# Encoder layer with two kinds of attention on one core: half strips in chunk two's projection, and local heads' scores and values held behind 512-column runs

## The chip, the core and the metric

The kernel runs on one core of a Trainium2 chip. The metric is the device time in microseconds (us); the median of several runs counts. TensorE (PE, with PEld for its weight loads), VectorE (DVE), ScalarE (ACT), GpSimd (POOL) and SyncE (SP, which issues the transfers here) each work through their own list of instructions in order.

## What is computed

```python
u = rms_norm(h, norm_w) @ w_in
qa, ka, va, za, qb, kb, vb, zb = split(u)
qa, ka = rope(rms_norm(qa, q_norm_a)), rope(rms_norm(ka, k_norm_a))
ya = global_gqa(qa, ka, va) * silu(za)                    # 8 heads, 2 of keys and values, all tokens
qb, kb = rms_norm(qb, q_norm_b), rms_norm(kb, k_norm_b)
yb = neighbourhood_attention(qb, kb, vb, rpb) * silu(zb)  # 8 heads, a window of 8 x 16 tokens and 16 meta tokens
return h + concatenate([ya, yb]) @ w_out
```

`h` has 2048 columns; there are a prompt of 1024 tokens and a sample of 256, each with the same 16 meta tokens in front. All inputs are float32.

## The kernel before

A float32 product is made of three matmuls of two-part operands: high by high, high by low, low by high. The input projection goes by **strips** of 128 output columns, 52 in all. A strip has 2048 / 128 = 16 steps `kt` over the input columns, and they are taken in four **quarters** `c` of four steps (`WCH = 4`). `strips` (from line 191) loads a quarter's weights (`wr`), splits them into `wh` and `wl` (ScalarE casts, VectorE subtracts; for some strips the low part is read back from an earlier chunk), and then issues its matmuls. `wh` and `wl` have four buffers each, `wr` three.

The tokens go through in two chunks. Chunk one has 512 tokens, one block. Chunk two (`chunk2`) has 784 tokens in two blocks: 512 columns (tile `x`) and 272 columns (tile `xb`). Per quarter each block has 4 steps x 3 = 12 matmuls, so that TensorE goes back and forth: 12 matmuls of 512 columns, 12 of 272, 12 of 512, and so on, four times a strip. Each block of a strip adds up in its own PSUM tile `pp` (four buffers), and is evacuated by `qk_evac`, `v_rows` or `z_evac`.

Among the strips of chunk two stands attention. First come the global heads (tiles `sp<-q,kf` for scores, `po<-ph,va` for values), issued by `run` behind the strips that they need; a strip of a local head follows each. Then come the other local strips, and in them the local heads: at the end of every second quarter, `run_due` issues what a table of places has for it, at most one block's scores (`scores`: lines 488, 315, 316) and one block's values (`values`: lines 519, 522), both in `attend_strip`. A block's values have their place two half strips behind its scores. Between them lie the masked scores on VectorE (L493), maxima (L502, L505, L326, and GpSimd L328), exponentials on ScalarE (L510, L513) and the meta tokens' probabilities `Pm` (L337, L338).

The order in which all of this stands on each engine is made by a scheduler that models the time of the instructions and keeps dependencies; `place_after` and `add_manual_dep` add an order where no data asks for one. The last strip of chunk two is **turned** (`self.turn`): its 272-column block goes first in each quarter. `tie` names the quarter and block behind which the transposes of the strip before (`v_turn`, `rows_out`, L543) may stand. Behind chunk two comes the output projection (`outproj`, lines 1073 to 1075), with the last local head's blocks in it.

Of the kernel before, what the change touches and what calls it, by code (L numbers as in the profile page):

```python
# [21 lines left out]
P = 128  # L22
# [26 lines left out]
WCH = 4  # L49
# [10 lines left out]
class Kern:  # L60
# [131 lines left out]
    def strips(self, jobs, getx):  # L192


        nc, tc = self.nc, self.tc
        out = [[pool.tile([P, 512], F32, tag=tag, name="pp") for pool, tag in pools] for _, _, pools in jobs]
        for c in range(KT // WCH):
            ws = []
            behind = self.behind.pop(0) if self.behind else None
            for j, (s, _, _) in enumerate(jobs):  # L200
                wp = self.w if j < 2 else self.w1
                with tc.high_priority(offset=self.woff), tc.issue_after(behind) if behind else nullcontext():
                    w = self.raw.tile([P, WCH, P], F32, tag="raw", name="wr")
                    cuts = ((0, 1), (1, WCH)) if self.projected == 3 and c == 0 and not self.second else ((0, WCH),)
                    for i, e in cuts:
                        self.lastw = nc.sync.dma_start(w[:, i:e], self.io["w_in"][s][:, c * WCH + i:c * WCH + e, :]).ins
                    wh = wp.tile([P, WCH, P], F32R, tag="wh", name="wh")
                    wl = wp.tile([P, WCH, P], F32R, tag="wl", name="wl")
                    if self.second and s not in AGAIN:
                        nc.sync.dma_start(wl[:].bitcast(F32), self.wld[s][:, c * WCH:(c + 1) * WCH, :])  # L210
                        nc.scalar.copy(wh[:], w[:])
                    else:
                        for i, e in cuts:
                            self.lastsplit = self.split(wh[:, i:e], wl[:, i:e], w[:, i:e])
                            self.lasthi = self.hi
                ws.append((wh, wl))
                if not self.second and s not in AGAIN:
                    nc.sync.dma_start(self.wld[s][:, c * WCH:(c + 1) * WCH, :], wl[:].bitcast(F32))
            nb = len(jobs[0][1])
            for b in range(nb)[::-1] if self.turn else range(nb):  # L220
                for k in range(WCH):
                    kt = c * WCH + k
                    xh, xl = getx(kt)[b]
                    first, last = kt == 0, kt == KT - 1
                    for (wh, wl), ps, (_, blocks, _) in zip(ws, out, jobs):
                        p, n = ps[b], blocks[b][1]
                        nc.tensor.matmul(p[:, :n], wh[:, k, :], xh[:, :n], start=first, stop=False)  # L227
                        nc.tensor.matmul(p[:, :n], wh[:, k, :], xl[:, :n], start=False, stop=False)  # L228
                        self.lastmm = nc.tensor.matmul(p[:, :n], wl[:, k, :], xh[:, :n], start=False, stop=last).ins  # L229
                if self.turned and (c, b) == self.tie:  # L230
                    for i in self.turned:
                        tc.add_manual_dep(i, self.lastmm.name, mybir.DependencyInfo(
                            mybir.DependencyClass.NoSync, mybir.DependencyReason.DATA), reason="turned")
                    self.turned = []
            if c % 2:
                self.run_due()
        return out

    def turn_ins(self, i):
        self.turned.append(i)  # L240

    def run_due(self):
        if self.late:
# [222 lines left out]
    def attend_strip(self, q, qf, zs, k, meta, vals, vmeta, tab, w, ydst):  # L466

        nc = self.nc  # L470
        qv = q[:].rearrange("p i (g r) -> p i g r", g=4)[:, :, :, 64 * w:64 * w + 64]
        qfv = qf[:].rearrange("p (g r) -> p g r", g=4)[:, :, 64 * w:64 * w + 64]
        groups = {0: (0, 2), 3: (2, 4), 1: (0, 3), 2: (1, 4)}
        pa = self.sp.tile([P, 2, QB], F32, tag="sp", name="sp")
        pb = self.sp.tile([P, 2, QB], F32, tag="sp", name="sp")
        sa = self.s.tile([P, 2, QB], F32, tag="S", name="S")
        sb = self.s.tile([P, 2, QB], F32, tag="S", name="S")
        pa, pb, sa, sb = (x[:].rearrange("p a b -> p (a b)") for x in (pa, pb, sa, sb))

        def part(a, b, t):  # L480

            return (a[:, :P], b[:, :192], b[:, 192:384], a[:, P:2 * P])[t]

        for t in (0, 3, 1, 2):
            a, e = groups[t]
            dst = part(pa, pb, t)
            o = 256 * t + 32 * WIN0[w]
            nc.tensor.matmul(dst, k[:, o:o + P], qfv[:, a:e, :], start=True, stop=True)  # L488
            if t == 3:
                sm = self.meta_scores(pa[:, 256:], meta, qv[:, 0], qv[:, 1], SCALE)  # L490
        ty = WTYPE[w]
        for x, y, n, o in ((sa, pa, 256, 64), (sb, pb, 384, 0)):
            nc.vector.scalar_tensor_tensor(out=x[:, :n], in0=y[:, :n], scalar=SCALE, in1=tab[:, ty, o:o + n],  # L493
                                           op0=ALU.mult, op1=ALU.add)

        def ap(t, off, dims):
            return bass.AP(t.tensor, t.offset + off, [list(t.ap[0])] + dims)

        def gather(name, op):

            m = self.t.tile([P, QB], F32, tag="t", name=name)
            nc.vector.tensor_tensor(out=ap(m[:], 0, [[128, 2], [64, 2], [1, 64]]), in0=ap(sa, 0, [[128, 2], [64, 2], [1, 64]]),  # L502
                                    in1=ap(sb, 0, [[128, 2], [192, 2], [1, 64]]), op=op)
            v = ap(m[:], 64, [[64, 2], [1, 64]])
            nc.vector.tensor_tensor(out=v, in0=v, in1=ap(sb, 64, [[192, 2], [1, 64]]), op=op)  # L505
            return m

        ma = self.all_max(gather("m1", ALU.max), sm)
        nc.vector.tensor_tensor(out=sa[:, :256], in0=sa[:, :256], in1=ma[:], op=ALU.subtract)
        nc.scalar.activation(sa[:, :256], sa[:, :256], AF.Exp)  # L510
        v = ap(sb, 0, [[192, 2], [1, 192]])
        nc.vector.tensor_tensor(out=v, in0=v, in1=ap(ma[:], 0, [[64, 2], [1, 192]]), op=ALU.subtract)
        nc.scalar.activation(sb[:, :384], sb[:, :384], AF.Exp)  # L513
        pm3 = self.meta_probs(sm, ma, 1.0)
        tot = self.mx.tile([P, 2, QB], F32, tag="mx", name="tot")[:, 0, :]
        self.all_sum(gather("a1", ALU.add), sm, tot)
        yield
        po = self.op.tile([P, 2, QB], F32, tag="po", name="po")[:, 0, :]
        nc.tensor.matmul(po, vmeta, pm3[:], start=True, stop=False)
        for t in (0, 3, 1, 2):  # L520
            a, e = groups[t]
            nc.tensor.matmul(po[:, 64 * a:64 * e], vals[:, t, :], part(sa, sb, t), start=False, stop=t == 2)  # L522
        self.put_y(po, tot, zs, ydst)
# [103 lines left out]
    def chunk1(self):  # L627
        nc, io = self.nc, self.io
        self.early_due, self.place = {}, 0
        self.due, self.late, self.turn, self.behind, self.turned, self.tie = iter(()), [], False, [], [], (1, 0)  # L630
        self.woff, self.second, self.projected, self.sums = 0, False, 0, self.w_sums()
        self.scale2 = [self.one2.tile([P, T2], F32, tag=n, name=n) for n in ("rb2", "eb2")]
        self.xsq, self.vlcopies, self.wouts = {}, [], 0
        self.start_chunk(T1)
# [102 lines left out]
        for g in range(2):  # L737
# [4 lines left out]
            else:  # L742
                k, = pr(k_strip(KA + g, g, kw, True))
# [6 lines left out]
        for h in range(8):  # L750
            kj, qj = kb_strip(KB + h, 2 + h, kwb), qb_strip(QB_ + h, 8 + h, qwb)
            k, = pr(kj)
# [15 lines left out]
    def chunk2(self):  # L768
        nc, io = self.nc, self.io
# [29 lines left out]
        def v_rows_of(s, g):  # L799

            def evac(ps):
                for p, (o, n) in zip(ps, BL):
                    self.rows_out(self.v_rows(p, o, n), n, self.vn[g], C1P + o)
            return s, BL, evac
# [141 lines left out]
        for g in range(2):  # L946
            if g == 0:
                k, _ = pr(k_strip(KA, 0, kw, True), v_rows_of(VA, 0))
                self.tie = 0, 1
            else:  # L950
                k, = pr(k_strip(KA + g, g, kw, True))
                pr(v_rows_of(VA + g, g))
            v = v_tiles(g)
            for h in range(4 * g, 4 * g + 4):
                z, = pr(z_strip(ZA + h, h) + (((self.sp, "sp"),) if h == 0 else ()))
                q, = pr(q_strip(QA + h, h, qw, True))
                run(h, q, z, k, v)
                fill(FILL)
# [390 lines left out]
```

## Time and profile before

| | |
|---|---|
| median of 3 runs | 2153.4 us (2153.36 to 2154.49) |
| profiled execution | 2154.02 us, its span 2152.2 us |
| TensorE busy | 2146.3 us |
| VectorE busy | 1675.4 us |
| ScalarE busy | 1204.0 us |
| GpSimd busy | 530.0 us |
| chain that ended last | 99% TensorE |

A matmul's row gives its start and how long it was in the engine. Neighbours overlap there, so the time that one takes from the engine is the distance from its start to the start of the next. A row with several instructions (x4, x8) has them merged.

### The profile page before, as it was taken

Reading aid. Unit: us, or ns where it says so; the run is one execution under the profiler, and the core shown is the slowest. Engines: PE = TensorE matmul, PEld = TensorE weight load, DVE = VectorE, ACT = ScalarE, POOL = GpSimd, SP = SyncE. Lnnn points to the kernel's source line nnn. Section 1 sums busy time; section 2 is a strip of 40 time slices with the busy share of each in tenths; the row PEclk is TensorE's granted clock in tenths of the full one; section 3 lists DMA queues with packets and bytes.
Section 4 is the critical chain, followed back from the end, with each engine's and each line's share of the span. In section 5 each row is a group of like instructions: output and inputs, shape, how many; then the busy total and the mean of one; then the engine's idle time right before and its main releaser. Section 6 shows DMA issues by size and latency. Waiting matters only on the chain.

```text
span 2152.2 us, 33487 instructions
## 1 busy us (share of the span) xinstructions
PE 2146.3 (100%) x11473; PEld 1866.0 (87%) x11473; DVE 1675.4 (78%) x3053; ACT 1204.0 (56%) x2459; POOL 530.0 (25%) x250
## 2 busy tenths in 40 slices
PE   9999999999999999999999999999999999999999
PEld 7888888888888899998998898989999888888887
DVE  7688987788874899898799898787787886545763
ACT  7677644554665777777677776444444454232230
POOL 1142422222221223232133413333333311000000
PEclk9999999999999999999999999999999999999999
DMA  8657799988654333334333334654433364762663
GB/s 294 215 186 228 242 295 319 348 280 271 212 190 133 99 100 108 109 108 125 100 105 101 106 119 128 206 162 139 133 123 124 114 214 144 241 235 89 235 226 107
DMA packets 257419, 377.21 MB, mean 175 GB/s; under 512 B 43072, under 2 KB 108768, under 8 KB 257248
## 3 DMA queue, kind: packets, MB, share of 16 engines
q1 hardware_dynamic: 257248, 375.07, 54.2%
q8 instruction: 90, 1.47, 0.3%
q14 instruction: 81, 0.66, 0.1%
HBM read 281.01 MB, written 100.38 MB: 177 GB/s over the span
## 4 chain that ended last, share of the span: by engine, by line
PE 99%; DMA 0%; DVE 0%; SPq 0%; issue 0%; ACT 0%
PE pp L227 22%; PE pp L229 22%; PE pp L228 22%; PE pq L1075 6%; PE pq L1074 6%; PE pq L1073 6%; PE po L422 3%; PE po L522 2%; PE sp L488 2%; PE sp L383 2%; PE sp L384 2%; PE sp L382 1%; PE po L423 1%; PE tp L543 0%; PE sm_ps L316 0%; PE sm_ps L315 0%
## 5 line engine op out<-in xcount | busy, mean ns | idle before, releaser
L227 PE MATMUL pp<-x,wh 128*128 128x512 f32 (+1 forms) x1664 | 654.4, 394 | 0.8 <-ACT wh L66 0.8
L228 PE MATMUL pp<-x,wh 128*128 128x512 f32 (+1 forms) x1664 | 648.3, 390 | 0.0
L229 PE MATMUL pp<-x,wl 128*128 128x512 f32 (+1 forms) x1664 | 648.2, 390 | 0.0
L229 PEld LDWEIGHTS pp<-x,wl 128*128 128x128 f32 x1664 | 312.6, 188 | 63.0 <-DVE wl L67 0.6
L227 PEld LDWEIGHTS pp<-x,wh 128*128 128x128 f32 x1664 | 312.6, 188 | 57.8 <-ACT wh L66 3.1
L228 PEld LDWEIGHTS pp<-x,wh 128*128 128x128 f32 x1664 | 312.9, 188 | 53.6
L262 POOL PARTITION_ALL_REDUCE m<-ms x78 | 237.8, 3049 | 324.5 <-ACT ms L260 251.2
L346 POOL PARTITION_ALL_REDUCE tot<-a x80 | 175.8, 2198 | 476.2 <-DVE a L343 449.2
L67 DVE TENSOR_TENSOR wl<-wr,wh 128x512 fp32r<-128x512 f32 (+2 forms) x287 | 212.6, 742 | 102.4 <-ACT wh L66 77.3
L66 ACT CAST wh<-wr 128x512 fp32r<-128x512 f32 (+2 forms) x287 | 174.0, 611 | 163.9 <-PE pp L228 148.9
L228 PE MATMUL pp<-xb,wh 128*128 128x272 f32 x832 | 240.6, 289 | 0.0
L227 PE MATMUL pp<-xb,wh 128*128 128x272 f32 x832 | 239.7, 288 | 0.0
L229 PE MATMUL pp<-xb,wl 128*128 128x272 f32 x832 | 239.4, 288 | 0.0
L1075 PE MATMUL pq<-wm,yl 128*128 128x512 f32 x560 | 218.5, 390 | 0.1
L1073 PE MATMUL pq<-wm,yh 128*128 128x512 f32 x560 | 218.5, 390 | 0.0
L1074 PE MATMUL pq<-wm,yh 128*128 128x512 f32 x560 | 218.2, 390 | 0.0
L328 POOL PARTITION_ALL_REDUCE ma<-m x80 | 109.1, 1364 | 424.7 <-DVE m L326 424.7
L228 PEld LDWEIGHTS pp<-xb,wh 128*128 128x128 f32 x832 | 156.5, 188 | 8.4
L227 PEld LDWEIGHTS pp<-xb,wh 128*128 128x128 f32 x832 | 156.6, 188 | 8.1
L229 PEld LDWEIGHTS pp<-xb,wl 128*128 128x128 f32 x832 | 157.5, 189 | 0.9
L1075 PEld LDWEIGHTS pq<-wm,yl 128*128 128x128 f32 x560 | 105.1, 188 | 22.3 <-DVE yl L67 0.5
L1073 PEld LDWEIGHTS pq<-wm,yh 128*128 128x128 f32 x560 | 105.2, 188 | 21.7
(217 smaller groups left out, 3879.3 us busy)
## 6 DMA issues: line engine op xcount, KB each, us to landing
wr<-in_w_in SPq DMA_DIRECT2D x413, 256.0 KB, 3.4
wld<-wl SPq DMA_DIRECT2D x132, 256.0 KB, 4.2
wl<-wld SPq DMA_DIRECT2D x132, 256.0 KB, 3.1
yr<-yd SPq DMA_DIRECT2D x35, 512.0 KB, 5.2
wq<-in_w_out SPq DMA_DIRECT2D x64, 256.0 KB, 5.1
td<-wq SPq DMA_DIRECT2D x64, 256.0 KB, 4.3
ww<-td SPq DMA_DIRECT2D x64, 256.0 KB, 5.4
ww<-in_w_out SPq DMA_DIRECT2D x48, 256.0 KB, 5.1
```

The lines of the kernel that those rows point to most:

```text
L66: self.hi = nc.scalar.copy(hi, full).ins
L67: return nc.vector.tensor_tensor(out=lo, in0=full, in1=hi.bitcast(F32), op=ALU.subtract).ins
L227: nc.tensor.matmul(p[:, :n], wh[:, k, :], xh[:, :n], start=first, stop=False)
L228: nc.tensor.matmul(p[:, :n], wh[:, k, :], xl[:, :n], start=False, stop=False)
L229: self.lastmm = nc.tensor.matmul(p[:, :n], wl[:, k, :], xh[:, :n], start=False, stop=last).ins
L262: nc.gpsimd.partition_all_reduce(m2[:], ms[:], P, RED.add)
L328: nc.gpsimd.partition_all_reduce(ma[:], m1[:], P, RED.max)
L346: nc.gpsimd.partition_all_reduce(tot[:], a1[:], P, RED.add)
L422: nc.tensor.matmul(po[:], vh, hl[:, i], start=j == 0, stop=False)
L1073: nc.tensor.matmul(ps, yh, wh, start=k == 0, stop=False)
L1074: nc.tensor.matmul(ps, yh, wl, start=False, stop=False)
L1075: self.lastmm = nc.tensor.matmul(ps, yl, wh, start=False, stop=k == 7).ins
```

## The change

In `strips`, a lone job with two blocks (chunk two's strips, the turned one excepted) no longer issues matmuls at an even quarter: it keeps the quarter's weights in `held`, and at the odd quarter goes through both quarters for the 512-column block, then through both for the 272-column block. So 24 matmuls of 512 columns are followed by 24 of 272.

`hold` takes note of instructions, outside the turned strip: the four windows' score matmuls of a local block (not the meta tokens' ones) and the first of its values' matmuls. In chunk two, behind the next 512-column run, `place_after` ties them to its last matmul, so that they stand behind it. `tie` becomes quarter 0, block 0 once the first strips are done, where it was block 1.

```diff
@@ strips
+        held = []
         for c in range(KT // WCH):
@@
             nb = len(jobs[0][1])
+            held.append((c, ws))
+            if nb > 1 and len(jobs) == 1 and c % 2 == 0 and not self.turn:
+                continue
             for b in range(nb)[::-1] if self.turn else range(nb):
-                for k in range(WCH):
-                    kt = c * WCH + k
+                for kt, ws in [(d * WCH + k, w) for d, w in held for k in range(WCH)]:
+                    k = kt % WCH
                     xh, xl = getx(kt)[b]
@@
-                if self.turned and (c, b) == self.tie:
+                if b == 0 and self.second and not self.turn:
+                    for i in self.held:
+                        self.place_after(i, self.lastmm, "whole run")
+                    self.held = []
+                if self.turned and (held[0][0], b) == self.tie:
@@
                     self.turned = []
+            held = []
             if c % 2:
                 self.run_due()
@@
+    def hold(self, i):
+        if not self.turn:
+            self.held.append(i.ins)
@@ attend_strip
-            nc.tensor.matmul(dst, k[:, o:o + P], qfv[:, a:e, :], start=True, stop=True)
+            self.hold(nc.tensor.matmul(dst, k[:, o:o + P], qfv[:, a:e, :], start=True, stop=True))
@@
-        nc.tensor.matmul(po, vmeta, pm3[:], start=True, stop=False)
+        self.hold(nc.tensor.matmul(po, vmeta, pm3[:], start=True, stop=False))
@@ chunk2
-                self.tie = 0, 1
+                self.tie = 0, 0
```

What it does to TensorE's order among the local heads, at a block's values; first before (`po` is the output, `S` and `Pm` probabilities, `vw` and `vm` values; L227 to L229 are the projection, and lines behind the edit are 4 to 13 higher after it):

```order
L228 MATMUL pp<-xb,wh 128x272
L229 MATMUL pp<-xb,wl 128x272
L519 MATMUL po<-Pm,vm_271 128x256
L522 MATMUL po<-S,vw 128x128 x2
L522 MATMUL po<-S,vw 128x192 x2
L227 MATMUL pp<-x,wh 128x512
L228 MATMUL pp<-x,wh 128x512
```

The same block after:

```order
L232 MATMUL pp<-x,wh 128x512
L233 MATMUL pp<-x,wl 128x512
L532 MATMUL po<-Pm,vm_271 128x256
L535 MATMUL po<-S,vw 128x128 x2
L535 MATMUL po<-S,vw 128x192 x2
L231 MATMUL pp<-xb,wh 128x272
L232 MATMUL pp<-xb,wh 128x272
```

The values moved from the border between a 272-run and a 512-run to that between a 512-run and a 272-run, and the runs around them became 24 long.

VectorE near the end of chunk two, where the block before the last head's blocks gets its probabilities `Pm`; before (`rs_r` is the evacuation of the last head's query strip, `q<-qfull` the split of its queries, loaded back from memory):

```order
L338 TENSOR_TENSOR Pm<-Sm,Pm 16x256
L355 TENSOR_TENSOR tot<-tot,r 128x256
L505 TENSOR_TENSOR a_19640<-a_19640,S 128x128
L280 SCALAR_TENSOR_TENSOR rs_r_19666<-pp,nqkw,rs_r_19666 128x272
L356 SCALAR_TENSOR_TENSOR r<-tot,r 128x256
L343 TENSOR_TENSOR a_19640<-a_19640,Sm 16x256
L368 TENSOR_TENSOR y<-y,r 128x256
L67 TENSOR_TENSOR wl<-wr,wh 128x512
L289 TENSOR_TENSOR vt<-pp,rb_320 128x512
L355 TENSOR_TENSOR tot<-tot,r 128x256
L356 SCALAR_TENSOR_TENSOR r<-tot,r 128x256
L67 TENSOR_TENSOR q<-qfull,q 128x1024
```

And after, one row behind the same evacuation of `rs_r` (L293 there):

```order
L339 TENSOR_TENSOR m_19625<-m_19625,Sm 16x256
L302 TENSOR_TENSOR vt<-pp,rb_320 128x512
L522 TENSOR_TENSOR S<-S,ma 128x256
L525 TENSOR_TENSOR S<-S,ma 128x384
L346 TENSOR_TENSOR Sm<-Sm,ma 48x256
L372 TENSOR_TENSOR y<-po,z 128x256
L515 TENSOR_TENSOR a_19640<-S 128x256
L518 TENSOR_TENSOR a_19640<-a_19640,S 128x128
L67 TENSOR_TENSOR q<-qfull,q 128x1024
L356 TENSOR_TENSOR a_19640<-a_19640,Sm 16x256
L67 TENSOR_TENSOR wl<-wr,wh 128x512
L351 TENSOR_TENSOR Pm<-Sm,Pm 16x256
```

`Pm` moved from ahead of the split of the queries to behind it, and the evacuation that feeds the queries moved ahead of this block's maxima.

## Rows read from the trace of the kernel before

**Rows 1.** The page: span, busy time of each engine, chain that ended last.

```profile
span 2152.2 us, 33487 instructions
PE 2146.3 (100%) x11473; PEld 1866.0 (87%) x11473; DVE 1675.4 (78%) x3053; ACT 1204.0 (56%) x2459; POOL 530.0 (25%) x250
...
PE 99%; DMA 0%; DVE 0%; SPq 0%; issue 0%; ACT 0%
```

**Rows 2.** Chunk two's two parts: length, busy time by engine, granted clock, transfers.

```profile
598.90:1352.50 753.60, 753.60 (x4564) 676.85 (x4563) 640.54 (x1183) 538.62 (x1100) 215.88 (x100) 1.00 0.39 117
1352.50:1756.65 404.15, 404.15 (x2422) 364.87 (x2420) 313.61 (x661) 185.57 (x419) 139.22 (x74) 1.00 0.47 146
```

**Rows 3.** Groups of TensorE in 598.9:1756.65: count, busy, mean ns, idle before.

```profile
L227 PE MATMUL pp<-x,wh 128*128 128x512 f32 x832 | 331.4, 399 | 0.0
...
L228 PE MATMUL pp<-xb,wh 128*128 128x272 f32 x832 | 240.6, 289 | 0.0
```

**Rows 4.** TensorE in order of time (start, length), local part, borders of runs.

```profile
1399.94 0.53 PE L227 MATMUL pp<-x,wh 128*128 128x512 f32 x1
...
1402.84 0.29 PE L227 MATMUL pp<-xb,wh 128*128 128x272 f32 x1
...
1404.33 0.39 PE L227 MATMUL pp<-x,wh 128*128 128x512 f32 x1
...
1407.08 0.29 PE L227 MATMUL pp<-xb,wh 128*128 128x272 f32 x1
```

**Rows 5.** The same view: 24 and 24 in the global part, 12 at the end.

```profile
625.71 0.39 PE L227 MATMUL pp<-x,wh 128*128 128x512 f32 x1
...
631.15 0.29 PE L227 MATMUL pp<-xb,wh 128*128 128x272 f32 x1
...
634.14 0.40 PE L227 MATMUL pp<-x,wh 128*128 128x512 f32 x1
...
1753.93 0.39 PE L227 MATMUL pp<-x,wh 128*128 128x512 f32 x1
...
1756.65 0.39 PE L1073 MATMUL pq<-wm,yh 128*128 128x512 f32 x1
```

**Rows 6.** The same view: 272-runs behind values and behind transposes.

```profile
1738.72 0.42 PE L227 MATMUL pp<-xb,wh 128*128 128x272 f32 x1
...
1740.37 0.40 PE L227 MATMUL pp<-x,wh 128*128 128x512 f32 x1
...
1743.13 0.29 PE L227 MATMUL pp<-xb,wh 128*128 128x272 f32 x1
...
1747.74 0.37 PE L227 MATMUL pp<-xb,wh 128*128 128x272 f32 x1
...
1749.34 0.40 PE L227 MATMUL pp<-x,wh 128*128 128x512 f32 x1
```

**Rows 7.** The same view: two blocks' scores and values; VectorE's last step for one.

```profile
1695.99 0.61 PE L488 MATMUL sp<-qfull,kfull 128*128 128x128 f32 x4
...
1716.88 0.28 PE L519 MATMUL po<-Pm,vm 128*128 128x256 f32 x1
...
1718.09 0.61 PE L488 MATMUL sp<-qfull,kfull 128*128 128x128 f32 x4
...
1736.21 0.41 DVE L338 TENSOR_TENSOR Pm<-Sm,Pm 16x256 fp32r<-16x256 f32 x1
...
1737.64 0.28 PE L519 MATMUL po<-Pm,vm 128*128 128x256 f32 x1
```

**Rows 8.** The same view: last reader of a weight buffer, and its next split.

```profile
1737.53 0.28 PE L229 MATMUL pp<-xb,wl 128*128 128x272 f32 x1
...
1745.85 0.69 DVE L67 TENSOR_TENSOR wl<-wr,wh 128x512 fp32r<-128x512 f32 x1
```

**Rows 9.** The same view: the last head's queries on ScalarE and VectorE.

```profile
1743.63 1.05 ACT L66 CAST q<-qfull 128x1024 fp32r<-128x1024 f32 x1 [1.78 <-DMA qfull<-q2d]
...
1744.71 1.23 DVE L67 TENSOR_TENSOR q<-qfull,q 128x1024 fp32r<-128x1024 f32 x1 [1.87 <-ACT q L66]
```

More of the change, by code (lines that the diff above doesn't have):

```diff
@@ L630, in chunk1 @@
         self.due, self.late, self.turn, self.behind, self.turned, self.tie = iter(()), [], False, [], [], (1, 0)
-        self.woff, self.second, self.projected, self.sums = 0, False, 0, self.w_sums()
+        self.woff, self.second, self.projected, self.sums, self.held = 0, False, 0, self.w_sums(), []
         self.scale2 = [self.one2.tile([P, T2], F32, tag=n, name=n) for n in ("rb2", "eb2")]
```

## The prediction

> **What bounds the kernel now.** I read the page first, then the busy time by stage, then the matmul groups, then the order of time at a few places. TensorE is busy for 2146.3 of 2152.2 us and the chain that ended last is 99% TensorE [rows 1]; a change that saves nothing on TensorE saves nothing. The second chunk runs from 598.9 to 1756.65 us. In its two parts (global heads' attention among the projections; local heads' attention among the projections) TensorE has no idle time at all, at a granted clock of 1.00, while VectorE is busy 85% and 78% of the time [rows 2], and none of the six projection groups has a wait before it [rows 3]. So the projection cannot lose waits here. What is left is the spacing of one matmul's start to the next, and the mean duration of one (399 and 289 ns) does not tell it, since neighbours overlap. The order of time tells it. Twelve 512-column matmuls behind a 272-column run take 1407.08 - 1404.33 = 2.75 us; twelve 272-column ones take 1404.33 - 1402.84 = 1.49 us [rows 4]. A 512-run that is already in step is quicker: 2.72 us for twelve (1753.93 to 1756.65), and 5.44 us for 24 (625.71 to 631.15) [rows 5]. So **each entry into a 512-run costs some 0.03 us**, in its first matmuls. A 272-run has no such entry: 24 take 2.99 us (631.15 to 634.14), 1.50 for twelve [rows 5].
>
> **The change, part by part.** The counts below are of the built order; instructions are the same, nothing is added or removed on TensorE, only moved.
>
> *Half strips instead of quarters.* 49 single strips x 2 half strips each drop one switch in either direction. Attention matmuls cut many runs anyway: counting maximal runs of 512-column projections, the global part goes from 218 to 186, the local part from 87 to 53.
> - Local part: 34 entries fewer x 0.03 = -1.0 us.
> - Global part: 32 fewer x 0.03 = -1.0 us at most; 512-runs there are often cut before an entry is paid in full, and cuts move at random, so I take -0.7, with 0 as the other end.
>
> *Scores and values held between the 512-run and the 272-run.* Before, they stand ahead of a 512-run (39 times in the local part), now ahead of a 272-run (37 times).
> - The entry into a 512-run behind scores: 1402.84 - 1399.94 = 2.90 us on record, but its first row is drawn over the tail of the score (0.53 against 0.39 us), so 2.90 - 0.14 = 2.76 [rows 4], 0.01 over an ordinary entry, 0.02 with the rounding of the record. Gone 39 times: between -0.8 and -0.4; I take -0.6.
> - A 272-run behind values is on record once: 1740.37 - 1738.72 = 1.65, less the same overlap (0.42 against 0.29), 1.52; behind transposes 1749.34 - 1747.74 = 1.60 less 0.08, again 1.52 [rows 6]. That is 0.02 over 1.50 for twelve, and no row shows the second twelve. Ends: 0.02 (it falls back into step) and 0.05 (it never does) for 24. I take 0.03, since in both rows the excess lasted the whole twelve but the second twelve is unseen: 37 x 0.03 = +1.1, ends +0.7 and +1.9.
> - The 512-run behind such a 272-run took 1743.13 - 1740.37 = 2.76 [rows 6], 0.01 over 2.75: 37 x 0.01 = +0.4 at most, 0 at least; I take +0.3.
>
> [...] The rows show 125 ns per 272-column matmul with its weight load (2.99 us / 24) and 127 ns behind short work (1.52 / 12). [...]
>
> *Waits.* Held instructions wait on nothing new in data. Behind a held one stand the next projections, so a late score or value now stops TensorE as it did before. Distances: scores of a block to its values are two half strips, before and after; the shortest is the last block of a head, 1737.64 - 1718.09 = 19.6 us, of which 1736.62 - 1718.09 = 18.5 us pass until its probabilities are written, 1.0 us to spare; others have 1716.88 - 1695.99 = 20.9 us [rows 7]. I take no stall: 0, with the price in the fourth case.
>
> *Weights.* Two of the four buffers are now read at once. A strip's quarter came to its split's end at 1746.54, 9.0 us after the last reader of its buffer started at 1737.53 and 7.4 us ahead of use [rows 5, 8], the longest such lag but one or two among 208. Now the even quarter's buffer is free 12 x 0.125 = 1.5 us before its half strip ends and is wanted one half strip later: 1.5 + 8.46 = 10.0 us at least. Covered, by 1.0 us; price 0. DMA queue: the same loads in nearly the same order on SyncE; stores and loads move past each other by one or two places. VectorE, ScalarE and GpSimd keep their work and have idle time. PSUM: the 512 block of a strip now ends 3.0 us ahead of the strip's end instead of 1.5, so its evacuation has more room.
>
> *Sum:* -1.0 - 0.7 - 0.6 + 1.1 + 0.3 = -0.9 us. The profiled execution took 2154.0 us (span 2152.2 and 1.8 around it), 0.6 above the median of 2153.4; taken from the median this is **2152.5 us**. All ends in the good direction: -1.0 - 1.0 - 0.8 + 0.7 = -2.1; in the bad one without stalls: -1.0 - 0.4 + 1.9 + 0.4 = +0.9. What a measurement of this kernel can tell from no change is 0.2%, 4.3 us. So the reordering alone stays inside it either way.
>
> **The rivals.**
> 1. *In step throughout.* The 272-runs behind scores fall into step at once, and every dropped switch pays, also where attention cuts: 98 x 0.03 = -2.9 us, 2150.5. For it: 24 in 2.99 us [rows 5]. Against: both rows behind short work. It would take entries of 0.045 us instead of 0.03 to pass 4.3 us, which no row shows.
> 2. *It doesn't do what it says:* the scheduler puts the held work elsewhere, or attention cuts the longer runs as often. The order shows the held groups at the border in 37 places and 34 of 87 local 512-runs gone, so only the global part can go that way, with 0 instead of -0.7: 2153.2.
> 3. [...] All 24 behind a score go at 127 ns: +1.9 instead of +1.1, the following entry +0.4, global 0: -1.0 - 0.6 + 1.9 + 0.4 = +0.7, 2154.1.
> 4. *Slower: values wait for probabilities.* Scores are now issued 5.5 us later against the evacuations of the strips, which share VectorE (78% busy) with them, and the 512 block's evacuation starts with them in every second half strip. If a chain grows from 18.5 us past 19.6, TensorE stands at the values. Seven heads have such a last block: with 2 us of growth 7 x (2 - 1.1) = 6.3 us, others have 2.4 us to spare and stay free: 2158.8. It decides from 1.0 us of growth on. For it: the small reserve. Against: in the order, the stretch of VectorE's list from a last block's masked scores to its probabilities holds 22 instructions where it held 21.
> 5. *Slower: tail and weights.* At the end, the last block's probabilities stand on VectorE behind the cast of the last head's queries, which waited for a load until 1743.63 [rows 9], and its values stand on TensorE in the third run of the last strip. If that load lands as late as before, TensorE waits until 1743.6 + 1.1 + 1.2 + 1.4 = 1747.3 instead of about 1743: +4 us. I expect the load some 6 us earlier, since the evacuation that feeds it now stands ahead of the block's maxima. A weight buffer that is late by 1 us four times costs the same. 2156.5.
>
> **How the numbers follow.** Forecast 0.55, rival 1 0.12, rival 2 0.07, rival 3 0.09, rival 4 0.10, rival 5 0.07. Below 2149.1 (faster by over 0.2%) lies only the end of rival 1, with a way of pairing that no row shows: 0.05. Above 2157.7 lie most of rival 4 and a third of rival 5, with stalls of both kinds together: 0.13. The rest, 0.82, is the same. The range runs from 2150.2 to 2157.5: it takes in both ends of the sum, rivals 1, 2 and 3 and most of rival 5, and leaves out rival 4 and what is beyond rival 1, 0.17 together.
>
> **What would show it.** Right: TensorE still without idle time from 598.9 us to the end of the second chunk; 24 of 512 columns in 5.47 us behind a 272-run; 24 of 272 columns behind values in 3.01 to 3.04 us (less: rival 1; 3.04: rival 3); the chunk's end 0.2 to 2 us earlier. Wrong: rows of values with a wait before them ended by VectorE or ScalarE (rival 4), a first 512-row waiting for a weight split, or a gap at the last block's values (rival 5). A shift of more than 3 us without any wait would mean that the cost of a switch is not what these rows say.

## The result: slower, by waits in the global heads' part

The changed kernel takes 2160.07 us in the median of 8 runs (2158.88 to 2161.09), the kernel before 2154.26 on the same chip (2153.32 to 2155.53). The ratio is 1.0028, with a 95% interval of 1.0019 to 1.0037. That is 5.8 us slower, where I had forecast 2152.5 us and no difference that can be measured; it also lies above my range, which ended at 2157.5. The profiled execution took 2158.88 us, 4.9 more than that of before.

The page of the changed kernel, beside [rows 1]: span, busy time of each engine, share of each engine in the chain that ended last.

```profile
span 2157.1 us, 33498 instructions
...
PE 2147.7 (100%) x11473; PEld 1866.9 (87%) x11473; DVE 1665.4 (77%) x3053; ACT 1203.6 (56%) x2459; POOL 537.7 (25%) x250
...
PE 94%; DVE 3%; DMA 2%; issue 0%; POOL 0%; ACT 0%; SPq 0%; DVEq 0%; POOLq 0%
```

The work on TensorE is the same: as many matmuls, and 1.4 us more of busy time. What is new is in the last line: the chain is no longer TensorE alone, VectorE has 3% of it. (That is the time for which the chain runs along VectorE's list, not the time that was lost.) The table of stages, beside [rows 2] (length, then busy time of TensorE, weight loads, VectorE, ScalarE, GpSimd, then the granted clock):

```profile
598.90:1352.50 753.60, 750.87 (x4533) 672.46 (x4532) 635.29 (x1174) 534.08 (x1096) 218.14 (x99) 1.00 0.37 115
1352.50:1757.00 404.50, 404.44 (x2423) 365.91 (x2422) 307.27 (x666) 187.17 (x417) 144.90 (x75) 1.00 0.48 147
```

TensorE was busy for all 753.60 us of the first stage before; now it stands idle for 2.7 of them, at the same clock, while the local part is full as before. TensorE's waits in the whole run (line, releaser: us in total, times, longest):

```profile
PE sp L395 <- ACT S L399: 2.2, 1, 2.2
PE pp L231 <- ACT wh L66: 1.2, 2, 0.8
PE warm L657 <- DVE wz L654: 1.2, 1, 1.2
PE po L435 <- DVE ph L67: 0.5, 2, 0.3
PE tp L309 <- DVE vm L67: 0.4, 1, 0.4
```

Scores (L395) and values (L435) of global heads wait for ScalarE and VectorE. In the kernel before the only waits were the warm-up's and 0.8 us in three at L227, for weights.

To share out all of the difference I use one tally for every kernel here. Over chunk two, each matmul's distance from its start to the next one's is compared with the usual distance of its kind (0.2266 us for 512 columns, 0.1245 for 272, taken from long runs). Single stretches of over 0.025 us beyond that count as waits, the rest is spacing. It sees more than the view of waits, which leaves out the matmul's tail.

| against before, us | global waits | local waits | 512-column spacing | 272-column spacing |
|---|---|---|---|---|
| changed kernel | +4.5 | +0.3 | -1.5 | +1.9 |

With what attention's own matmuls shift by a little, this is +5.2; a wait of 0.4 at the start of the output projection went away, which leaves the 4.9 us of the spans. So the reordering costs some 0.4 us, and the waits the rest.

The longest wait, engine by engine: TensorE, then what each other engine did (start, length, idle time before it).

```profile
836.12 0.39 PE L231 MATMUL pp<-x,wh 128*128 128x512 f32 x1
838.67 0.39 PE L395 MATMUL sp<-q,kf 128*128 128x256 f32 x1 [2.16 <-ACT S L399]
...
837.71 0.42 ACT L66 CAST q<-rs_r 128x272 fp32r<-128x272 f32 x1 [2.85 <-DVE rs_r L290]
838.04 0.58 ACT L399 COPY S<-sp 128x512 f32<-128x512 f32 x1
...
834.87 0.41 DVE L380 TENSOR_TENSOR y<-y,z 128x256 f32<-128x256 f32 x1
835.20 2.48 DVE L290 TENSOR_TENSOR rs_r<-t,rs_r 128x272 f32<-128x272 f32 x1
837.60 0.41 DVE L381 SCALAR_TENSOR_TENSOR y<-y,r 128x256 f32<-128x256 f32 x1
...
835.10 3.27 POOL L275 PARTITION_ALL_REDUCE m<-ms  x1
```

Read it from the bottom. GpSimd begins a strip's sum of squares at 835.10 and is at it until 838.37. VectorE begins a multiply of another strip at 835.20, one that takes 0.42 to 0.44 us at seven of its ten places, and holds on to it for 2.48, until 837.68. ScalarE wants its result for a rounding (L66) and waits 2.85 us. Behind that, in ScalarE's list, stands the copy of earlier scores out of PSUM (L399), which waits for nothing else. TensorE's next scores need that PSUM tile and wait 2.16 us. Four engines in a row, each in its own list's order; the rounding and the copy have nothing to do with each other.

In the kernel before the sum of the same strip begins 1.2 us earlier and meets another step of VectorE, and nobody is hurt:

```profile
833.45 4.54 DVE L402 TENSOR_TENSOR S<-S,ma 128x512 f32<-128x512 f32 x4
837.91 0.41 DVE L333 TENSOR_TENSOR Sm<-Sm,ma 48x256 f32<-48x256 f32 x1
838.25 0.42 DVE L277 TENSOR_TENSOR rs_r<-t,rs_r 128x272 f32<-128x272 f32 x1
...
833.90 3.33 POOL L262 PARTITION_ALL_REDUCE m<-ms  x1 [1.48 <-ACT ms L260]
```

There a subtraction of scores was stretched (four take 4.54 us instead of about 2.5), which had time to spare, and the multiply (L277, 0.42 us) came after the sum. In chunk two, 104 VectorE steps of before are stretched by over 0.15 us (85 us in all), and 84 of the changed kernel (73 us); every one of them lies under a GpSimd sum or maximum. So the changed kernel has fewer collisions, not more. What differs is where they fall: at 836 us on a chain to TensorE that has no room.

### The profile page after: what moved, and what is told of

Same layout as the page of the kernel before. It is cut to its first block, busy times and chain, and to the rows that moved or that the text cites. A ratio compares the mean times of both kernels' runs of the same rounds, so it can differ in the third digit from the quotient of the medians.

```text
span 2157.1 us, 33498 instructions
## 1 busy us (share of the span) xinstructions
PE 2147.7 (100%) x11473; PEld 1866.9 (87%) x11473; DVE 1665.4 (77%) x3053; ACT 1203.6 (56%) x2459; POOL 537.7 (25%) x250
## 4 chain that ended last, share of the span: by engine, by line
PE 94%; DVE 3%; DMA 2%; issue 0%; POOL 0%; ACT 0%; SPq 0%; DVEq 0%; POOLq 0%
PE pp L231 21%; PE pp L232 21%; PE pp L233 21%; PE pq L1086 6%; PE pq L1087 6%; PE pq L1088 6%; PE po L435 3%; PE po L535 2%; PE sp L501 2%; PE sp L395 1%; PE sp L397 1%; PE sp L396 1%; PE po L436 1%; DMA wld<-wl 1%; DMA td<-wq 0%; PE tp L556 0%
## 5 line engine op out<-in xcount | busy, mean ns | idle before, releaser
L275 POOL PARTITION_ALL_REDUCE m<-ms x78 | 230.8, 2959 | 361.7 <-ACT ms L273 305.0
L67 DVE TENSOR_TENSOR wl<-wr,wh 128x512 fp32r<-128x512 f32 (+2 forms) x287 | 207.7, 725 | 79.7 <-ACT wh L66 59.8
L66 ACT CAST wh<-wr 128x512 fp32r<-128x512 f32 (+2 forms) x287 | 173.6, 611 | 153.4 <-PE pp L232 129.5
L231 PE MATMUL pp<-xb,wh 128*128 128x272 f32 x832 | 245.5, 295 | 0.0
L232 PE MATMUL pp<-xb,wh 128*128 128x272 f32 x832 | 240.0, 288 | 0.0
L341 POOL PARTITION_ALL_REDUCE ma<-m x80 | 120.4, 1505 | 413.7 <-DVE m L339 400.6
```

The source lines that it names most:

```text
L66: self.hi = nc.scalar.copy(hi, full).ins
L67: return nc.vector.tensor_tensor(out=lo, in0=full, in1=hi.bitcast(F32), op=ALU.subtract).ins
L275: nc.gpsimd.partition_all_reduce(m2[:], ms[:], P, RED.add)
L341: nc.gpsimd.partition_all_reduce(ma[:], m1[:], P, RED.max)
```

## The experiments

Theory: the loss sits in the global part alone; the new order there puts a VectorE step under a GpSimd sum where it reaches TensorE. Rivals: the half strips as such take the room away; or the local part's holding and order cost the time.

**One part of chunk two at a time.** `halved` and `holding` switch the two parts of the change on, by stage.

```diff
-            if nb > 1 and len(jobs) == 1 and c % 2 == 0 and not self.turn:
+            if self.halved and nb > 1 and len(jobs) == 1 and c % 2 == 0 and not self.turn:
@@ hold
-        if not self.turn:
+        if self.holding and not self.turn:
@@ e1: local part alone
+        self.halved, self.holding = False, True
@@ global heads
-                self.tie = 0, 0
+                self.tie = 0, 1
@@ behind the global heads
+        self.halved, self.tie = True, (0, 0)
```

e1_local has half strips and holding from the local heads on, and the global part of before: up to 1249 us TensorE's list is the same, row by row.

> Half strips and the hold only from the first local head's scores on; up to there every engine's order is that of the kernel before. Theory (the loss is made of TensorE's waits in the global heads' part): no wait over 0.1 us before 1320 us, the whole within +1.0 us of the kernel before (some +0.3 from 272-column runs behind scores, +0.3 from a wait at the last block's values). Rival (the loss is the new order itself, spread over all of chunk two): +2.5 us or more, half of the loss of the changed kernel.

Measured: 2154.29 us against 2153.65, ratio 1.0004 (0.9995 to 1.0013).

e2_global has half strips in the global part alone, and holds nothing.

```diff
-        self.halved, self.holding = False, True
+        self.halved, self.holding = True, False
@@ global heads
-                self.tie = 0, 1
+                self.tie = 0, 0
@@ behind the global heads
-        self.halved, self.tie = True, (0, 0)
+        self.halved, self.tie = False, (0, 1)
```

> Half strips only in the global heads' part, nothing held; up to the local heads every engine's order is that of the changed kernel. Theory: +4.5 to +5.5 us against the kernel before, with the same waits at the same places (a wait of about 2.2 us at a score near 838 us). Rival (the order itself, spread): +2.5 us, with no wait needed for it.

Measured: 2159.13 us, ratio 1.0028 (1.0017 to 1.0040), with the changed kernel's waits, one after the other, 0.7 us earlier: again 2.2 us at the scores (L395) and 0.5 in two at the values (L435). So the whole loss is in the global part, and the local part is level with before.

**Half strips in the local part without holding** (against e1).

```diff
-        self.halved, self.holding = False, True
+        self.halved, self.holding = False, False
```

> Half strips only in the local heads' part, scores and values left where they fall (between a 272-column run and a 512-column run). Theory: 34 entries into 512-column runs fewer, none of the 272-column runs behind scores: -1.0 us against the kernel before and 1.3 us under the run with the hold. Rival (holding is what pays, or the place is of no account): the same as the run with the hold, or slower.

Measured: 2158.58 us, ratio 1.0023 (1.0013 to 1.0032). I had missed what holding is good for. Its spacing was what I expected (-1.3 us for 512 columns, none for 272), but TensorE's waits in it read:

```profile
PE po L532 <- DVE Pm L351: 2.8, 2, 2.0
PE tp L556 <- DVE vt L302: 2.2, 1, 2.2
...
PE pq L1090 <- DVE yl L67: 1.1, 2, 0.9
```

Local values (L532) wait for the meta tokens' probabilities `Pm`, as in my rival 4. In the tally, 6.2 us of local waits and 1.8 behind chunk two. From scores to values it is 19.4 to 21.7 us in e3 and 19.6 to 21.7 in e1, behind the first block, so holding does not stretch that distance. But of the two blocks that wait, the probabilities come 20.3 and 21.5 us after the scores, and in e1 14.4 and 19.6: held scores and values stand otherwise to the strips' evacuations, and VectorE gets round to the probabilities sooner. Holding pays for waits that the half strips would bring.

**Moving the sum.** The changed kernel, in which GpSimd's sum of that one strip waits until the multiply is done; every engine's list is the same, instruction for instruction, and one semaphore's value is different. (The lines that pick out this one multiply are left out.)

```diff
-        nc.gpsimd.partition_all_reduce(m2[:], ms[:], P, RED.add)
+        g = nc.gpsimd.partition_all_reduce(m2[:], ms[:], P, RED.add).ins
+        if self.second and self.before_sum:
+            self.tc.add_manual_dep(g, self.before_sum.name, mybir.DependencyInfo(
+                mybir.DependencyClass.Sync, mybir.DependencyReason.DATA), reason="multiply first")
```

> The changed kernel with one number changed: GpSimd's sum for the third local query strip waits for two more VectorE instructions, the last being the multiply that took 2.48 us while the sum ran. Order of every engine unchanged. Theory (VectorE's step is stretched because GpSimd's sum runs at the same time, and TensorE waits for it by way of ScalarE's list): the multiply takes 0.4 to 0.5 us, the wait of 2.2 us before the score near 838 us is gone or under 0.5 us, and the whole is 1.5 to 2.5 us under the changed kernel. Rival (the score waits for PSUM or ScalarE anyway): the multiply gets short but the wait stays, no gain.

Measured: 2159.68 us, ratio 1.0028 (1.0017 to 1.0039): no gain. The place itself did what was expected of it (VectorE, then GpSimd):

```profile
834.92 0.43 DVE L294 TENSOR_TENSOR rs_r<-t,rs_r 128x272 f32<-128x272 f32 x1
835.27 0.41 DVE L387 SCALAR_TENSOR_TENSOR y<-y,r 128x256 f32<-128x256 f32 x1
835.61 2.73 DVE L421 TENSOR_TENSOR S<-S,ma 128x512 f32<-128x512 f32 x1
...
835.51 3.27 POOL L275 PARTITION_ALL_REDUCE m<-ms  x1 [0.69 <-issue]
```

The sum, which began 0.10 us ahead of the multiply, now begins 0.59 us behind its start, the multiply (here L294) takes 0.43 us instead of 2.48, and TensorE's wait at 836 falls from 2.33 to 0.28 us in the tally. That the stretch under the sum caused this wait is thereby shown. But now the sum falls on the subtraction of scores (2.73 us), as it did before the change, and later steps come late in turn:

```profile
843.89 0.50 PE L441 MATMUL po<-ph,va 128*128 128x512 f32 x1 [0.22 <-DVE ph L67]
846.59 0.37 PE L334 MATMUL sm_ps<-q,km 128*112 128x256 f32 x1 [0.53 <-DVE mx L411]
849.63 0.50 PE L441 MATMUL po<-ph,va 128*128 128x512 f32 x1 [0.67 <-DVE ph L67]
```

Global waits in the tally: 5.3 us, 4.5 before the edit. VectorE is busy for 635 of the 754 us of the global part; here the sum that was moved off one step landed on another.

**Other orders of the global part.** What is left is whether half strips take the room away, or this order of theirs is an unlucky one. `tie` is one pair of numbers that says behind which run the transposed values may stand; moving it changes the scheduler's order on all engines.

```diff
@@ e7_tie: the kernel before (quarters)
-                self.tie = 0, 1
+                self.tie = 0, 0
@@ e10_half_tie01: the changed kernel
-                self.tie = 0, 0
+                self.tie = 0, 1
@@ e12_half_tie20: the changed kernel
-                self.tie = 0, 0
+                self.tie = 2, 0
```

> The kernel before, quarters and nothing held, with one number altered: in the global heads' part the transposed values are tied one run earlier (behind the 512-column run of a strip's first quarter instead of the 272-column one). 1421 rows of TensorE's list and 548 of VectorE's move against before. Theory A (the loss of the change is a draw: a new order of the global part puts some VectorE step under a GpSimd sum where a wait reaches TensorE): this too costs something, 0.5 to 5 us, all of it as waits in the global part before steps that VectorE or ScalarE end, with VectorE steps three to five times as long under a GpSimd sum ahead of them; 2154.2 to 2159. Theory B (it is the half strips that take the slack of the global part): quarters keep it, no wait, 2153.7 within 0.5.

> The changed kernel with the tie of the global part moved from the 512-column run of the first half strip to its 272-column run; half strips and holding as in the change. 1244 rows of TensorE's list move against it. Theory A (a draw): the waits at 831 to 849 us move or vanish, the time falls anywhere from 2154.5 to 2162. Theory B (half strips as such): 4 to 5 us of waits in the global part again, at the same places (scores and values of local index 10 to 12), 2159 to 2160.5.

> The changed kernel with the tie of the global part one half strip later (the second half strip's 272-column run comes first, tie behind its 512-column run). A second draw of the same kind: 1898 rows of TensorE's list move. Theory A: 2154.5 to 2162, and not the same waits as the changed kernel; Theory B: 2159 to 2160.5 with waits at the same places.

| us | median | ratio, 95% interval | global waits | local waits |
|---|---|---|---|---|
| before, same chip | 2153.50 | 1 | 0 | 0 |
| e7: quarters, other tie | 2155.24 | 1.0007 (0.9998 to 1.0016) | 1.1 | 0.4 |
| e10: half strips, other tie | 2154.99 | 1.0007 (0.9998 to 1.0016) | 0.7 | 0.3 |
| e12: half strips, third tie | 2161.24 | 1.0035 (1.0022 to 1.0048) | 5.2 | 2.2 |

TensorE's waits in e10 and in e12 (lines as in the changed kernel):

```profile
PE warm L657 <- DVE wz L654: 1.2, 1, 1.2
PE pp L231 <- ACT wh L66: 0.9, 2, 0.5
```

```profile
PE po L532 <- DVE Pm L351: 1.8, 2, 1.0
...
PE sp L395 <- DVE Sm L333: 1.0, 2, 0.6
...
PE sp L395 <- ACT S L399: 0.7, 1, 0.7
PE po L435 <- DVE ph L67: 0.7, 2, 0.4
```

e10 has the whole change, half strips and holding in both parts, and no long wait: it cannot be told from before, and it is 4.5 us faster than the changed kernel by the ratios. Half strips as such do not cost the 5.8 us. With three places of one tie the same change costs 1.5 (not clear of noise), 5.8 and 7.7 us by the medians, with the long waits at other places each time; one of 0.4 to 0.7 us before values between 1184 and 1189 us is in all three. With quarters, the moved tie brings 1.5 us of waits where there had been none, the longest behind a VectorE step of 2.36 us (1219 us, 0.4 elsewhere) under a sum; its time cannot be told from before. The changed kernel's order is one of the worse ones, and that of before was one without a wait. `tie` is itself a line of the change, and e10 has it at the value of the kernel before.

e10 also shows what it takes besides a stretched step. The same multiply of the same strip falls under the same sum there (VectorE and GpSimd, then ScalarE and TensorE):

```profile
832.41 2.47 DVE L290 TENSOR_TENSOR rs_r<-t,rs_r 128x272 f32<-128x272 f32 x1
832.34 3.23 POOL L275 PARTITION_ALL_REDUCE m<-ms  x1
...
835.24 0.58 ACT L399 COPY S<-sp 128x512 f32<-128x512 f32 x1
...
835.04 0.40 PE L231 MATMUL pp<-x,wh 128*128 128x512 f32 x1
...
836.89 0.28 PE L395 MATMUL sp<-q,kf 128*128 128x256 f32 x1
```

ScalarE's copy stands behind the rounding as in the changed kernel (which waits 2.13 us here) and ends at 835.82. But the 512-run begins 2.7 us behind the sum's start, 1.0 in the changed kernel, and TensorE's next scores stand behind eight of its matmuls, where they stood behind one. They come at 836.89 without a wait.

**What holding does in the local part.** Half strips there alone, with the values held and the scores not (against e1).

```diff
-            self.hold(nc.tensor.matmul(dst, k[:, o:o + P], qfv[:, a:e, :], start=True, stop=True))
+            nc.tensor.matmul(dst, k[:, o:o + P], qfv[:, a:e, :], start=True, stop=True)
```

> Half strips in the local heads' part alone, values held as in the change, scores not held. Without any holding the local part lost 7.8 us to waits of values for probabilities and of the last transposes, though its order alone was 1.6 us quicker; with both held it had no such wait and was level with before. If it is the holding of the values that gives the probabilities time (2.7 us more from scores to values), the waits at the values go: 2153.5 to 2154.5. If scores that stay ahead of the 512-column run upset VectorE's order for the evacuations in any case, waits of 2 us at values and at the last transposes remain: 2156 to 2158.

Measured: 2153.15 us, ratio 0.9997 (0.9989 to 1.0006). (The values come 25 to 28 us behind the scores, 6 more than with both held; the 2.7 that I expected was half of it.) The spacing is better too, 272-columns +0.6 instead of +1.6 us: of the 20 full 272-runs behind values 11 are in step here. One long wait is left, at the last block's values. ScalarE and TensorE there:

```profile
1737.42 1.05 ACT L66 CAST q<-qfull 128x1024 fp32r<-128x1024 f32 x1 [2.78 <-DMA qfull<-q2d]
1738.37 0.41 ACT L347 ACTIVATE Sm<-Sm 48x256 f32<-48x256 f32 x1
...
1740.64 0.36 PE L532 MATMUL po<-Pm,vm 128*128 128x256 f32 x1 [1.40 <-DVE Pm L351]
```

The block's exponential (L347) stands behind the rounding of the last head's queries, which waits 2.78 us for a load; that is rival 5's order. e13 puts the two roundings of those queries behind the block's probabilities. (The lines that note these as `lastpc` and `lastpm` are left out.)

```diff
-            self.split(q[:, 0, :], q[:, 1, :], qf[:])
+            lo = self.split(q[:, 0, :], q[:, 1, :], qf[:])
+            if h == NH + 7:
+                self.place_after(self.hi, self.lastpc, "queries behind")
+                self.place_after(lo, self.lastpm, "queries behind")
```

> The kernel with half strips in the local part and values alone held, whose single long wait (1.4 us at the last block's values, 1740.6) stood behind the rounding of the last head's queries on ScalarE and VectorE, which waited 2.8 us for their load. Here these two instructions stand behind the last block's probabilities on both engines; nothing else moves but a dozen matmuls there. If that order is the cause (rival 5 of the prediction), the wait goes and nothing late takes its place, since the queries are wanted 17 us later: 1.4 to 1.6 us less, 2151.3 to 2152.0 against 2153.5 of before. If the load or TensorE's turned half strip was the limit anyway, the wait stays and the time is 2153 again.

Measured: 2152.95 us against 2154.21, ratio 0.9994 (0.9985 to 1.0003). The wait at 1740 us is gone. Of those that are left only 0.2 us are in chunk two, at an earlier head's scores (1377 us):

```profile
PE pp L231 <- ACT wh L66: 1.3, 2, 0.9
PE warm L658 <- DVE wz L655: 1.2, 1, 1.2
PE sp L329 <- DVE q L67: 0.2, 1, 0.2
```

It is the lowest ratio of the study, with quarters in the global part, half strips in the local part and only the values held; but it cannot be told from the kernel before. Nor is the gain that I expected shown: against e11 it is 0.6 us by the ratios, where I had said 1.4 to 1.6.

**Holding alone** (e5, against e1): quarters throughout, scores and values held.

```diff
-        self.halved, self.tie = True, (0, 0)
+        self.halved, self.tie = False, (0, 1)
```

> Quarters as before, with local scores and values held behind the next quarter's 512-column run: the holding alone. It adds no entry into a 512-run and takes none away, and lets 272-column runs follow short work. By the spacing in the two kernels with half strips in the local part, with and without holding, the 272-column matmuls lose 1.6 us in all (2.86 against 1.23), and the 512-column ones gain or lose no more than 0.3: 2154.8 to 2155.2 without new waits (before 2153.5). My forecast's price would be +1.1 and -0.6, 2154.0. Should holding bring waits by itself, they stand at the values behind VectorE's probabilities, and the time is above 2156.

Measured: 2154.30 us, ratio 1.0002 (0.9993 to 1.0010), no new waits, spacing +0.8 us for 272 columns and -0.2 for 512. I had expected +1.6 for the 272-runs, and carried the price of a run of 24 over to runs of 12, which lose half of it.

## Why the prediction was wrong

**The step that failed is "Waits. ... I take no stall: 0".** It looked at the local part alone, at scores and values that keep their distance. The runs showed 4.8 us of waits on TensorE in chunk two where there had been none, 4.5 of them in the global part and 2.3 at one place. For the other engines one sentence stood under "Weights", that they "keep their work and have idle time". Both halves of it were true and not enough. VectorE's work is not a fixed time, since steps stretch from 0.4 to 2.5 us under GpSimd's sums, and whether a step does is decided by the order: in e6 a shift of 0.7 us between the two was enough. And in e10 the same stretch does no harm, since TensorE's list has more left to do ahead of the scores. I had counted that the global part's runs fall from 218 to 186, so that its order moves throughout, and had priced that at TensorE's switches only. The moved `tie`, one of the change's lines, had no term at all; with it left at 0, 1 the same change is 4.5 us faster (e10). The trace of before showed what was at stake: over a hundred stretched steps in chunk two, with not one wait behind them. A state without any wait, on engines that are 85% and 78% busy [rows 2], is a thing that a new order can only lose. None of my rivals had a wait in the global part.

**Entries into 512-runs, local: right.** Forecast -1.0 us, measured -1.3 (e3's spacing against before).

**Entries, global: the other end of the range.** Forecast -0.7, with 0 as the other end. In e2 the 512-column spacing gains 0.45 us, and about as much goes back, 0.29 in 272-runs and the rest in attention's own matmuls.

**Holding: mis-sized.** I took -0.6 for entries behind scores, +0.3 for entries behind a slow 272-run and +1.1 for the slow 272-runs. From e3 to e1, which differ in holding alone, the first two make nothing that the tally can tell from 0 together, and the third is some +1.6. The rows: a 272-run behind held scores, from its first row to the 512-run behind it and on to the next scores, in the changed kernel.

```profile
1389.05 0.42 PE L231 MATMUL pp<-xb,wh 128*128 128x272 f32 x1
...
1392.22 0.40 PE L231 MATMUL pp<-x,wh 128*128 128x512 f32 x1
...
1397.71 0.61 PE L501 MATMUL sp<-qfull,kfull 128*128 128x128 f32 x4
```

24 matmuls take 1392.22 - 1389.05 = 3.17 us, less the 0.13 by which the first row is drawn over the tail of the score, 3.04. That is 127 ns for each, all the way, in 22 of 22 full runs behind scores and 8 of 8 behind values; a run of 36 takes 4.70 us, 4.57 less the same overlap, and has not come back either. In step it is 2.99 [rows 5], and so again in e3. So what I took as unseen, the second twelve, is as slow as the first, and the price of rival 3 was the right one. The 512-run behind it takes 1397.71 - 1392.22 = 5.49 us, 0.02 over my 5.47; the 33 full ones take 5.48 in the median. In the sum, the reordering makes about +0.4 us where I had -0.9: it stays inside what can be measured, as I had said.

**Rival 4 (values wait for probabilities): right in its mechanism, wrong in what brings it.** I had put it down to the held scores. It is the half strips that bring it, and the holding that takes it away (e3, e1), down to one wait of 0.3. My threshold held: in e3's last block the probabilities come 21.5 us behind the scores, 18.5 in before, and more than 1 us of growth is a wait. It came in two blocks, where I had priced seven.

**Rival 5 (the last block's values): there, but small.** In the changed kernel the last queries' load ended at 1743.6, not 6 us earlier as I thought, and the probabilities came behind it:

```profile
1744.70 1.23 DVE L67 TENSOR_TENSOR q<-qfull,q 128x1024 fp32r<-128x1024 f32 x1 [3.31 <-ACT q L66]
...
1746.88 1.21 DVE L351 TENSOR_TENSOR Pm<-Sm,Pm 16x256 fp32r<-16x256 f32 x1
```

But the whole block moved back too, its values to 1748.23, 19.7 us behind its scores, with the probabilities 19.6 behind them. So 0.3 us were lost instead of 4; 0.8 of the second row are again a stretch under a GpSimd sum (1746.34 to 1748.51). With the scores not held the values came at 1740.64 and lost 1.4 us, until the order was changed (e13).

**"A shift of more than 3 us without any wait"** did not come: the shift is made of waits, as the list of what would show me wrong had it for local values, at lines it did not name.

What stays open: for the other waits in the global part (849, 1188 us, those of e12) a stretched step lies ahead on VectorE in most cases, but only the one at 836 us was taken away to see it go. And a global order with half strips that has no wait at all was not found among three.

## What to carry to other kernels

Where the bound engine has no idle time and the engines that feed it are 80% busy, an edit that makes a scheduler reorder a stage has a price of its own, of several us here, on top of what it is meant to do. Look in the trace of before for steps whose length varies several times over at one shape, count them, and give a new order a chance to put one on a chain that reaches the bound engine. Before blaming an idea, try it with another order: one number moved this kernel by 4.5 us with the idea in it.

## What the runs showed of the chip

**Which VectorE steps stretch.** In the kernel before, 280 VectorE steps began under a GpSimd sum or maximum early enough to have ended 0.6 us before it did. Of the 214 whose inputs all lie in SBUF 119 were stretched by over 0.15 us, in the changed kernel 115 of 226; of those with an input in PSUM none of 66, and none of 76. All in a row, in the changed kernel (VectorE, then GpSimd):

```profile
1076.21 0.68 DVE L421 TENSOR_TENSOR acc<-acc,S 128x512 f32<-128x512 f32 x1
1076.81 0.67 DVE L403 TENSOR_TENSOR mx<-S,sp 128x512 f32<-128x512 f32 x1
1077.41 2.13 DVE L421 TENSOR_TENSOR acc<-acc,S 128x512 f32<-128x512 f32 x1
...
1076.04 3.94 POOL L275 PARTITION_ALL_REDUCE m<-ms  x1 [5.89 <-ACT ms L273]
```

The maximum that reads `sp` from PSUM passes in 0.67 us; the next sum of two SBUF tiles takes 2.13, until 1079.54, 0.44 us before GpSimd's end at 1079.98. The stretched steps end 0.43 us before the end of GpSimd's row in the median. The Trainium skill names a cause, in "SBUF — State Buffer", "Who interferes with whom": a VectorE instruction with two SBUF inputs contends with a GpSimd instruction that reads SBUF, and the one that comes second is blocked fully. The trace agrees on which steps can be hit; the ports themselves no run here shows. It differs on how long: the page has the pair of ports held for the whole instruction, but the first step above passed within GpSimd's row, in 0.68 us, as 95 of the 214 did.

**A 272-run keeps the pace with which it begins.** In the local part of the changed kernel all 22 full runs behind scores and all 8 behind values go at 127 ns a matmul to their end, where 125 is usual behind 512-columns. It is no rule of all short work: in e11, 11 of the 20 full runs behind values are in step, at 125, and 9 go at 127, again to the end. An in-step one there, behind values and up to the next scores:

```profile
1404.94 0.42 PE L231 MATMUL pp<-xb,wh 128*128 128x272 f32 x1
...
1408.07 0.61 PE L501 MATMUL sp<-qfull,kfull 128*128 128x128 f32 x4
```

It takes 3.13 us, 3.00 less the overlap. What decides between the two paces no run here tells. A 512-run behind short matmuls is in step after its first twelve (e3: 5.62 us for 24, 2.90 of them for the first twelve, 0.14 of these the overlap).
